# Weight loads of two mixers issued from GpSimd's queue instead of SyncE's

## The chip, the cores and the metric

The program runs on one core of one Trainium2 chip. The metric is the device time of one execution in microseconds; lower is better. The kernel before took 2750.52 us (median of three runs, 2747.89 to 2755.91).

## What is computed

A diffusion backbone of two layers on 1024 latent tokens and 256 context tokens, 1024 wide. Each layer has a mixer (layer 0: windowed attention beside a gated spatial unit; layer 1: latent attention beside a short gated convolution), and then 16 experts, each of which takes the tokens that score highest for it. Cut to the core:

```python
for layer in range(DEPTH):
    m_lat = split((silu(c) @ mod_w[layer] + mod_b[layer])[:, None], 6)      # the modulation
    h = rms_norm(x, norm1_g[layer]) * (1 + m_lat[1]) + m_lat[0]
    y = even_mixer(h, ...) if layer % 2 == 0 else odd_mixer(h, ...)         # projections, attention, output product
    x = x + m_lat[2] * y
    h = rms_norm(x, norm2_g[layer]) * (1 + m_lat[4]) + m_lat[3]
    x = x + m_lat[5] * expert_choice_ffn(h, router_w[layer], w1[layer], w3[layer], w2[layer])
return rms_norm(x, final_g)
```

In layer 0 the context tokens go the same way; in layer 1 they only give keys and values.

## The kernel before

Four stages follow each other: the mixer of layer 0 (`even`, 0 to about 690 us), its experts (to about 1430 us), the mixer of layer 1 (`odd`, to about 2160 us) and its experts. Every weight is loaded as fp32 and split into two fp16 parts (`split_w`, L101: ScalarE writes the high part, VectorE the low one), and products are three fp16 matmuls (`mm3`, L145).

**Queues.** SyncE (SP in the profile) issues two kinds of DMA. One is the bulk loads of weights: `load_split` (L110), the modulation's slabs in `mod_bank` (L205, L208), the experts' first slabs in `first_slabs` (L428), the output weights of layer 1 (L1150), and the experts' other slabs in `slab` (L452). The other is the transposes by DMA (`turn`, L152) of keys, queries, probabilities and outputs, which the mixers need between VectorE and TensorE, and in layer 1 the row loads `fetch` (L1298). GpSimd (POOL) issues the row loads of the first norm (L273) and of the tails (L295), the tails' stores (L311, L316) and the gathers and scatters of the experts; and while the tokens are being chosen it computes the low half of the experts' first slabs itself (`split_first`, L439). Each engine takes its queue in order: an instruction that waits holds up those behind it.

**Order.** The mixers are written as generators that `weave` (L56) advances side by side, and the framework plans each engine's order from a simulated timeline when the kernel is built (L36). A load is planned as early as its buffer is free, unless it is tied: `behind` (L190; "what is traced inside is issued after ins, on its engine") ties the slabs of bank 1 of layer 0 behind `loaded`, the last of the first weights, which SyncE loads (L204, L880), and L1310 ties the experts' slabs 4 to 10 of layer 1 behind the row load of the last tile, which SyncE loads as well:

```python
with tc.issue_after(K["ld"].ins):
    self.first_slabs(1, FS, 11)
```

**Layer 0.** Bank 0 of the modulation (16 slabs of 512 KB) comes first, then `wkv`, `wz` and `sgu_wT`. Then, beside the tiles' norms, projections and attention, banks 1 and 2 in three buffers `c4`, and `ev_wo`. When the projections are done, `then0` issues four expert slabs of 1 MB, and bank 0 of layer 1 follows in eight slabs of 1 MB (`mods1`, L894). Meanwhile VectorE chooses the tokens (`topk`, L345): a first half over tiles 0 to 5 (`r`), and a second half over tiles 6 and 7 (`l`), which needs the affinities that the tail of tile 7 copies at L341; then the context's choice.

**Layer 1.** Low-rank projections of ten tiles beside banks 1 and 2 of the modulation, convolution (24 loads of `wconv`, four of `od_wo`) beside attention, the tails of eight tiles, the choice beside the splits of eleven expert slabs.

Of the kernel before, what the change touches and what calls it, by code (L numbers as in the profile page):

```python
# [22 lines left out]
P = 128  # L23
# [32 lines left out]
def weave(*streams):  # L56
    """streams: (generator, expected sum of its yields, start); advances the one that is least far, start and length 1 being
    where and how fast it runs against the others; a stream that yields a function waits until it is true"""
    live = [[st[0], 0.0, float(st[1]), st[2] if len(st) > 2 else 0.0, None] for st in streams]
    while live:  # L60
        s = min((v for v in live if v[4] is None or v[4]()), key=lambda v: v[3] + v[1] / v[2])
        try:
            r = next(s[0])
            s[4] = r if callable(r) else None
            s[1] += 0.0 if callable(r) else r
        except StopIteration:
            live.remove(s)


class Tag:  # L70
    """one tag of a pool with a fixed number of buffers"""
# [8 lines left out]
class Net:  # L80
    def __init__(self, nc, tc, I, out, dbg=None):
        self.nc, self.tc, self.I, self.out, self.dbg = nc, tc, I, out, dbg or {}
        self.V, self.S, self.T, self.G, self.Y = nc.vector, nc.scalar, nc.tensor, nc.gpsimd, nc.sync

# [6 lines left out]
    def first(self, g, n):  # L91
        """the generator's instructions before the n traced ahead of them that are ready too"""
# [12 lines left out]
    def load_split(self, src, n, sp, raws, step=1024):  # L105
        """src [128, n] in DRAM -> sp [128, 2, n]"""
        for o in range(0, n, step):
            m = min(step, n - o)
            raw = raws([P, step], "raw")
            self.loaded = self.Y.dma_start(raw[:, :m], src[:, o:o + m]).ins  # L110
# [28 lines left out]
    def stats(self, x, n, junk, tag):  # L139
        """1 / rms of the rows; tag: buffers of its own for each caller that runs beside others"""  # L140
# [9 lines left out]
    def turn(self, dst, src):  # L150
        """dst [128, n, 128] <- the n blocks of src [128, n * 128] transposed, 2-byte elements"""
        return self.Y.dma_start(dst, src, transpose=True)  # L152

    def trans(self, src, n, psum, w=P):
        """src [128, n*w] fp32 -> psum tiles [w, 4, 128]"""
# [34 lines left out]
    def behind(self, ins):  # L190
        """what is traced inside is issued after ins, on its engine"""
        return contextlib.nullcontext() if ins is None else self.tc.issue_after(ins)

    def mod_bank(self, l, i, psum, raws, last=None, n=1024):
        """rows 32g + stream of the bank: columns 512(4i + g) of the modulation of layer l; n: columns of a load"""
# [3 lines left out]
        for k in range(9):  # L199
            for c in range(0, 2048, n):  # L200
                slab = raws([P, n], "mslab")
                cols = slice(i * 2048 + c, i * 2048 + c + n)
                if k < 8:
                    with self.behind(last and last[0]):  # L204
                        self.Y.dma_start(slab, I["mod_w"][l, k * P:(k + 1) * P, cols])  # L205
                    lhs, rows = self.cs[:, k, :], P
                else:
                    self.Y.dma_start(slab[0:1], I["mod_b"][l:l + 1, cols])  # L208
# [11 lines left out]
    def mod_cols(self, l, i, g0, psum):  # L220
        """chunks g0, g0 + 1 of a bank with the model's dimension on partitions: psum [128, 4, 128], columns 32(g0 + g) + stream"""
        return self.trans(self.modsb[l, i], 4, psum)[0]

    def mod_AB(self, l, which, psum):
        """per-partition gain and shift [128, 8] of the norm before the mixer (1) or before the experts (2)"""
# [19 lines left out]
    def router(self, l, j, A, B, psum):  # L245
        """router weights with the norm's gain in them, and the row that its shift gives"""
# [12 lines left out]
    def mod_bc(self, l, m, j, dst, psum):  # L259
        """row m of the modulation for stream j on all partitions, over WS"""  # L260
# [7 lines left out]
    def norm_T(self, src, l, j, hi, lo, xs, psum):  # L268
        """hi, lo: [128, 8, 128] views"""
# [18 lines left out]
    def tail(self, l, j, t, src, catT, wout, m2, xd, h2d, aff, psum, c4, t2, cn=None, xin=None, ptr=None):  # L288
        """catT: k -> (hi, lo) [128, 128 tokens]; wout: (k, half) -> (hi, lo); yields its tensor-engine time"""
# [55 lines left out]
    def topk(self, src, n, cap, tag, off=0, alt=None, bufs=0):  # L345
        """largest cap of src [16, n] in falling order and their columns plus off; src is used up; alt: a second buffer, which
        lets the search for columns run beside the next round"""
# [20 lines left out]
    def merge(self, r, l):  # L368
        """largest 128 of two falling lists of 128; on equal values the first list wins"""
# [10 lines left out]
    def slots(self, vals, idf, cap, psum, halves):  # L380
        """per slot: row index and gate [slots, 16]; halves: also the index of half rows, for both halves"""
# [25 lines left out]
    def ring(self, raws, spls, first=()):  # L407
        """buffers for the experts' weights as loaded and split, (pool, tag) of each, no pool: self.ep; first: those for the first loads"""
# [13 lines left out]
    def first_slabs(self, l, a, b):  # L422
        """loads of the weights a .. b before the tokens are chosen"""
        src = [s for e in range(2) for s in [self.I[n][l, e, fh, kh] for fh in range(2) for n in ("w1", "w3") for kh in range(2)]
               + [self.I["w2"][l, e, q] for q in range(4)]]
        for i in range(a, b):
            raw = self.raw()
            self.Y.dma_start(raw, src[i])  # L428
            self.ahead.append((raw, None))

    def split_first(self, a, b, last=None):
        """their split, beside VectorE, which the choice holds; not before the instruction last"""
# [9 lines left out]
    def slab(self, src, a):  # L442
        """128 x 2048 weights, split: two views [128, a, 2048 / a]"""
# [14 lines left out]
    def experts(self, l, xd, h2d, lat, ctx, hook=None, keep=None, out=None):  # L458
        """lat = (idx, gate, _); ctx = (xdc, h2dc, (idx, gate, idx2)) or None"""
# [7 lines left out]
        def halves(name, i, e):  # L467
            """[128, 8, N] for expert e, in self.ep or in a buffer of the pool keep"""
# [42 lines left out]
        def rows(fh, w1, w3, xh, xl, gh, gl):  # L511
            """512 of the hidden columns with the tokens on partitions, then transposed and split"""
# [87 lines left out]
    def norm_out(self, xs, fg, tag):  # L600
        """the rows of the tiles over their rms, times the gain, in place"""
# [16 lines left out]
    def even(self, xd, xdc, h2d, h2dc, then):  # L618
        nc, tc, V, S, T, G, Y, I = self.nc, self.tc, self.V, self.S, self.T, self.G, self.Y, self.I
        with self.pool("m0") as pm, self.pool("m0p", PSUM) as pp:  # L620
# [25 lines left out]
            with self.pool("m0i") as pi:  # L646
# [18 lines left out]
                loaded = self.loaded  # L665

# [10 lines left out]
            def ropes(ps, H, t):  # L677
                """rotated [128, H, 64] fp32, scale undone by the table"""
# [75 lines left out]
            def score(keep, u):  # L754
                """scores of the unit's heads, a bank for each run of blocks, and the transposed probabilities"""
# [38 lines left out]
            def values():  # L794
                """the oldest unit's probabilities times values; after a tile's last ones its heads' outputs"""
# [681 lines left out]
```

## Time and profile before

| | |
|---|---|
| median of three runs | 2750.52 us |
| lowest, highest | 2747.89, 2755.91 us |
| span of the profiled execution | 2750.4 us |
| TensorE, VectorE, ScalarE, GpSimd busy | 2361.6, 2036.0, 1678.1, 337.3 us |

The page gives the profiled execution's span, 2750.4 us, and no time of its own beside it; what lies around the span is therefore taken as nothing, and the span stands 0.1 us under the median. An engine's busy time is the sum of its instructions; idle time before an instruction is put down to what released it. "SPq" is SyncE's queue: it has no busy time, but the time that its instructions took to issue is shown.

### The profile page before, as it was taken

The page shows a single profiled execution, that of the slowest core. Times are in us where ns is not written, and L with a number is a line of the kernel's source. Part 1 is how long each engine was busy: PE and PEld are TensorE (multiplying, and loading weights), DVE is VectorE, ACT ScalarE, POOL GpSimd, SP SyncE. Part 2 cuts the span into 40 slices and gives each one's busy share as a digit, 9 for nine tenths or more (in the row PEclk, how much of TensorE's full clock was granted, in tenths as well). Part 3 has the DMA queues.
Part 4 walks back from the last instruction along what each step waited for, and adds up shares of the span by engine and source line. Part 5 has one row for each costly group of instructions (what it writes and reads, how often), then busy time and mean ns, then how long its engine had stood idle before and what let it go on. Part 6 is the DMA issues. An engine that isn't in the chain of part 4 may idle for free. (4 is left out here: it accounts for less than half of the span.)

```text
span 2750.4 us, 48542 instructions
## 1 busy us (share of the span) xinstructions
PE 2361.6 (86%) x19075; PEld 1436.0 (52%) x19075; DVE 2036.0 (74%) x3886; ACT 1678.1 (61%) x2750; POOL 337.3 (12%) x198
## 2 busy tenths in 40 slices
PE   5889888864899999999989989988884699999995
PEld 1345555432677777776855645544553244444442
DVE  5466666676677777767857768778778789888887
ACT  4355556514666676767745456656554588777774
POOL 1000000003111111111120000000015111112211
PEclk8999999886899999999999999999986799999998
DMA  8775555473788888887967657878876499999997
GB/s 309 218 171 118 123 106 117 93 260 112 267 307 285 323 286 322 289 319 272 352 204 225 147 124 142 152 137 186 162 187 244 181 371 401 361 366 360 373 370 273
DMA packets 461995, 661.32 MB, mean 240 GB/s; under 512 B 371115, under 2 KB 371419, under 8 KB 411077
## 3 DMA queue, kind: packets, MB, share of 16 engines
q1 hardware_dynamic: 439894, 582.81, 66.8%
q0 software_dynamic: 21872, 75.41, 9.4%
q8 instruction: 149, 2.44, 0.4%
q14 instruction: 80, 0.66, 0.1%
HBM read 526.86 MB, written 41.94 MB: 207 GB/s over the span
## 5 line engine op out<-in xcount | busy, mean ns | idle before, releaser
L103 DVE SCALAR_TENSOR_TENSOR spl<-raw,spl 128x2048 f16<-128x2048 f32 x369 | 831.7, 2285 | 149.4 <-ACT spl L102 148.8
L102 ACT ACTIVATE spl<-raw 128x2048 f16<-128x2048 f32 x369 | 690.5, 1910 | 191.7 <-DMA raw<-in_w 73.0
L146 PE MATMUL pb<-xsh,spl 128*128 128x160 f16 x1024 | 222.6, 239 | 0.0
L148 PE MATMUL pb<-xsh,spl 128*128 128x160 f16 x1024 | 222.2, 239 | 0.0
L147 PE MATMUL pb<-xsl,spl 128*128 128x160 f16 x1024 | 222.1, 239 | 0.0
L146 PE MATMUL pa<-xsh,spl 128*128 128x160 f16 x1024 | 215.9, 234 | 0.0
L147 PE MATMUL pa<-xsl,spl 128*128 128x160 f16 x1024 | 215.7, 234 | 0.0
L148 PE MATMUL pa<-xsh,spl 128*128 128x160 f16 x1024 | 215.6, 234 | 0.0
L146 PEld LDWEIGHTS <-spl 128*128 128x128 f16 x2048 | 204.0, 100 | 7.2 <-PE yc L590 5.1
L148 PEld LDWEIGHTS <-spl 128*128 128x128 f16 x2048 | 204.2, 100 | 0.2
L147 PEld LDWEIGHTS <-spl 128*128 128x128 f16 x2048 | 204.0, 100 | 0.2
L146 PE MATMUL y<-spl,gh 128*128 128x512 f16 x512 | 195.2, 383 | 10.2 <-ACT gh L114 10.2
L147 PE MATMUL y<-spl,gh 128*128 128x512 f16 x512 | 195.1, 382 | 0.0
L148 PE MATMUL y<-spl,gl 128*128 128x512 f16 x512 | 189.3, 385 | 4.9 <-DVE gl L116 4.9
L579 POOL DMA_INDIRECT xd<-ysb,idxl x31 | 125.4, 4044 | 529.2 <-DVE ysb L572 503.6
L1212 ACT ACTIVATE pr<-sps,nm 128x512 f32<-128x512 f32 (+1 forms) x192 | 116.7, 611 | 104.2 <-DVE nm L1203 79.5
L146 PE MATMUL po<-vS,pT 128*128 128x64 f16 x976 | 121.9, 198 | 56.7 <-DMA pT<-ps 34.6
L1195 PE MATMUL sps<-kT,qT 128*128 128x512 f16 (+1 forms) x576 | 133.7, 352 | 11.6 <-ACT pr L1212 11.2
L146 PEld LDWEIGHTS <-pT 128*128 128x128 f16 x976 | 92.1, 101 | 89.9 <-DMA pT<-ps 48.6
L1196 DVE TENSOR_REDUCE mx<-sps 128x1 f32<-128x512 f32 (+1 forms) x192 | 112.6, 596 | 33.9 <-PE sps L1195 30.9
L116 DVE TENSOR_TENSOR ps<-pr,ps 128x512 f16<-128x512 f32 (+1 forms) x192 | 111.8, 595 | 34.6 <-ACT ps L114 34.4
L213 PE MATMUL modps<-mslab,cs 128*2 128x512 f32 x384 | 89.4, 681 | 53.1 <-DMA mslab<-in_mod_w 48.6
(439 smaller groups left out, 5957.1 us busy)
## 6 DMA issues: line engine op xcount, KB each, us to landing
raw<-in_w SPq DMA_DIRECT2D x384, 1024.0 KB, 7.6
mslab<-in_mod_w SPq DMA_DIRECT2D x80, 512.0 KB, 5.8
mslab<-in_mod_w SPq DMA_DIRECT2D x8, 1024.0 KB, 9.5
raw<-in_wz SPq DMA_DIRECT2D x12, 512.0 KB, 6.7
raw<-in_wconv SPq DMA_DIRECT2D x24, 256.0 KB, 3.6
xin<-in_x POOLq DMA_DIRECT2D x8, 512.0 KB, 6.1
raw<-in_ev_wo SPq DMA_DIRECT2D x8, 512.0 KB, 3.9
xres<-in_x POOLq DMA_DIRECT2D x8, 512.0 KB, 5.3
```

The lines of the kernel that those rows point to most:

```text
L102: self.S.activation(hi, raw, AF.Copy, scale=scale)
L103: self.V.scalar_tensor_tensor(lo, raw, scale, hi, op0=OP.mult, op1=OP.subtract)
L116: self.V.tensor_tensor(lo, src, hi, OP.subtract)
L146: self.T.matmul(ps, lh, rh, start=first, stop=False)
L147: self.T.matmul(ps, lh, rl, start=False, stop=False)
L148: return self.T.matmul(ps, ll, rh, start=False, stop=last).ins
L213: T.matmul(ps[c0:c0 + 2], lhs, slab[:rows, g * 512:(g + 1) * 512], start=False, stop=(k == 8), tile_position=(0, c0))
L579: G.indirect_dma_start(out=xd, out_offset=IOA(ap=lat[0][:, e:e + 1], axis=0), in_=ysb, in_offset=None, compute_op=OP.add)
L1195: T.matmul(ps[:, :w], qT[:, 4 * j + h % 4], kT[:, k, c0:c0 + w], start=j == 0, stop=j == 2)
L1196: V.tensor_reduce(mx[:, i:i + 1], ps[:, :w], axis=AX.X, op=OP.max)
L1212: S.activation(pr[:, :w], sp[i][:, :w], AF.Exp, bias=nm, scale=SC1, accum_out=dn[:, i:i + 1])
```

## The change

A field `bulk` names the engine that issues the bulk loads. It is SyncE at the start, GpSimd from the point in `even` where the first weights have been issued to the end of that mixer, and GpSimd again in the whole of `odd`. The experts' `slab` and `early`, the row loads `fetch` and the transposes stay on SyncE. (Comments are also taken out.)

```diff
         self.V, self.S, self.T, self.G, self.Y = nc.vector, nc.scalar, nc.tensor, nc.gpsimd, nc.sync
+        self.bulk = self.Y
...
     def load_split(self, src, n, sp, raws, step=1024):
-            self.loaded = self.Y.dma_start(raw[:, :m], src[:, o:o + m]).ins
+            self.loaded = self.bulk.dma_start(raw[:, :m], src[:, o:o + m]).ins
...
     def mod_bank(self, l, i, psum, raws, last=None, n=1024):
                     with self.behind(last and last[0]):
-                        self.Y.dma_start(slab, I["mod_w"][l, k * P:(k + 1) * P, cols])
+                        self.bulk.dma_start(slab, I["mod_w"][l, k * P:(k + 1) * P, cols])
-                    self.Y.dma_start(slab[0:1], I["mod_b"][l:l + 1, cols])
+                    self.bulk.dma_start(slab[0:1], I["mod_b"][l:l + 1, cols])
...
     def first_slabs(self, l, a, b):
-            self.Y.dma_start(raw, src[i])
+            self.bulk.dma_start(raw, src[i])
...
     def even(self, xd, xdc, h2d, h2dc, then):
                 loaded = self.loaded
+            self.bulk = G
...
+        self.bulk = Y
         return lat_slots[0], ctx
...
     def odd(self, ms, mw, xs, xsc, xd, h2d, W, then):
+        self.bulk = G
...
-                            Y.dma_start(raw, I["od_wo"][q])
+                            self.bulk.dma_start(raw, I["od_wo"][q])
...
             K["mo"].__exit__(None, None, None)
+            self.bulk = Y
             return r
```

## Rows read from the trace of the kernel before

**Rows 1.** The page's first lines: span, busy time of each engine.
```profile
span 2750.4 us, 48542 instructions
PE 2361.6 (86%) x19075; PEld 1436.0 (52%) x19075; DVE 2036.0 (74%) x3886; ACT 1678.1 (61%) x2750; POOL 337.3 (12%) x198
```
**Rows 2.** Busy time by stretch: PE, PEld, DVE, ACT, POOL; then PEclk, DMA share, GB/s.
```profile
555.00:629.00 74.00, 53.00 (x322) 24.50 (x322) 50.55 (x123) 12.56 (x23) 3.19 (x6) 0.84 0.68 234
...
2045.00:2122.00 77.00, 48.44 (x219) 28.75 (x217) 64.58 (x128) 43.59 (x38) 35.86 (x14) 0.72 0.71 283
```
**Rows 3.** TensorE's waits, 105 to 200 us: total, times, longest (us).
```profile
PE modps L213 <- DMA mslab<-in_mod_w: 4.0, 4, 2.1
```
**Rows 4.** TensorE's waits, 555 to 629 us.
```profile
PE modps L213 <- DMA mslab<-in_mod_w: 17.6, 1, 17.6
```
**Rows 5.** TensorE's waits, 1432 to 1600 us.
```profile
PE modps L213 <- DMA mslab<-in_mod_w: 17.6, 5, 9.4
PE kvps L146 <- DMA ckT<-hk: 9.1, 2, 6.9
```
**Rows 6.** DMA issues: queue, count, KB each, median us from issue to landing.
```profile
mslab<-in_mod_w SPq DMA_DIRECT2D x80, 512.0 KB, 5.8
xin<-in_x POOLq DMA_DIRECT2D x8, 512.0 KB, 6.1
xx<-xd SPq DMA_DIRECT2D x8, 512.0 KB, 3.6
```
**Rows 7.** SyncE's queue in order of time: start, us to issue.
```profile
48.51 0.33 SPq L110 DMA_DIRECT2D raw<-in_sgu_wT  x1
48.88 1.38 SPq L205 DMA_DIRECT2D mslab<-in_mod_w  x3
...
554.82 2.31 SPq L428 DMA_DIRECT2D raw<-in_w  x4
...
557.75 11.63 SPq L152 DMA_TRANSPOSE pT<-p  x1
...
1400.35 0.90 SPq L110 DMA_DIRECT2D raw<-in_wconv  x2
...
1586.56 1.21 SPq L152 DMA_TRANSPOSE ckT<-hk  x1
...
2080.36 0.33 SPq L1298 DMA_DIRECT2D xx<-xd  x1
```
**Rows 8.** DMA traffic of the first 31 us.
```profile
DMA packets 3211, 10.96 MB, mean 354 GB/s; under 512 B 495, under 2 KB 543, under 8 KB 3211
```
**Rows 9.** VectorE in order of time: start, duration, in brackets idle before.
```profile
602.34 0.21 DVE L365 TENSOR_SCALAR tkir<-tkir 16x128 f32<-16x128 uint32 x1
...
624.82 0.17 DVE L329 TENSOR_REDUCE rnm<-lg 128x1 f32<-128x16 f32 x1 [14.31 <-PE lg L327]
...
628.82 0.28 DVE L341 COPY aff<-affps 16x128 f32<-16x128 f32 x1 [2.96 <-PE affps L340]
...
1586.07 0.43 DVE L116 TENSOR_TENSOR hk<-ck,hk 128x256 f16<-128x256 f32 x1 [0.48 <-ACT hk L114]
...
2088.02 1.27 DVE L306 SCALAR_TENSOR_TENSOR xx<-yps,xx 128x512 f32<-128x512 f32 x2
```
**Rows 10.** GpSimd in order of time, start of layer 1's mixer.
```profile
1438.18 1.06 POOL L273 DMA_DIRECT2D xin<-xc  x2 [2.85 <-DMA xc<-y,idx]
```
**Rows 11.** Groups by line, 2045 to 2122 us, GpSimd and VectorE: count, busy us, mean ns.
```profile
L439 POOL TENSOR_TENSOR spl<-raw,spl 128x2048 f16<-128x2048 f32 x8 | 32.6, 4070 | 39.1 <-ACT spl L438 39.1
L129 DVE SCALAR_TENSOR_TENSOR rstt<-rstt,mst 128x1 f32<-128x1 f32 x9 | 8.5, 948 | 0.1
L334 DVE TENSOR_SCALAR re<-re,rden 128x16 f32<-128x16 f32 x3 | 7.3, 2423 | 0.1
```
**Rows 12.** The rows of tile xin, 1432 to 1560 us: count, ns least/median/most.
```profile
L275 DVE TENSOR_SCALAR xin<-xin,rstdn x10: 745/753/755, 1445.4 to 1546.0; 128x1024 f32<-128x1024 f32 x10
...
L273 POOL DMA_DIRECT2D xin<-xd x8: 527/528/530, 1452.1 to 1532.9; - x8
```

## The prediction

> **What bounds the kernel now.** I read the page's busy times first: TensorE is busy for 86% of the span, VectorE for 74%, and GpSimd, which is to take the loads, for 12% [rows 1]. That share is an average, so I went by stretches next. The experts, more than half of the span, are not touched; what counts is when each mixer hands its choice of tokens to them. Two stretches of the mixers are not TensorE's: in 555 to 629 us, where layer 0 chooses, TensorE is busy for 53.00 of 74 us, and in 2045 to 2122 us, where layer 1 chooses, for 48.44 of 77, while VectorE has 64.58 [rows 2]. Then I read TensorE's waits in the stretches where bulk loads run, since a load or a transpose that comes sooner is worth at most the wait that it ends. They are small: 4.0 us for slabs in 105 to 200 us [rows 3], 17.6 us in one piece in the choice of layer 0 [rows 4], and 17.6 and 9.1 us in the projections of layer 1 [rows 5]. All together 48.3 us, 1.8% of the span, bounds the whole gain from above.
>
> **What moves.** 139 DMAs change queues: 60 in layer 0 (32 slabs of 512 KB and 4 rows of bias, 8 of `ev_wo`, 7 expert slabs, 8 slabs and a row of bias of bank 0 of layer 1) and 79 in layer 1 (36 for banks 1 and 2, 4 `wuq`, 24 `wconv`, 4 `od_wo`, 11 expert slabs). The bytes and the 16 engines that move them stay. A row load costs GpSimd 0.53 us to issue [rows 12], so 139 make 74 us on an engine that is idle for 88% of the span; I cost the issue itself at nothing, covered by that idleness, and at 0.53 us for each load that stands directly before a store or a split that is already due. SyncE gets its issue times back and then holds transposes and the row loads `fetch` alone. On GpSimd's queue the loads are moved in beside the norms' row loads, the tails' stores and, in the choices, the splits. Step by step:
>
> (a) Start. The slabs of bank 1 were tied behind the last first weight, on SyncE: three of them follow it at once, at 48.88 us [rows 7]. The tie holds only on the engine of its argument, so on GpSimd it is gone, and a load goes out when its buffer is free: two `wconv` loads went out at 1400.35 us, some 180 us before the next ones [rows 7]. The three `c4` buffers are free from the start and GpSimd is idle then. So 3 x 524 KB = 1.57 MB join the first 31 us, in which the DMAs moved 354 GB/s [rows 8] and bank 0 is what TensorE waits for: 1.57 MB / 354 GB/s = 4.4 us at most, 0 at least (they might be planned later). I take +3.5, near the upper end, because the row at 1400.35 shows the habit.
>
> (b) Banks 1 and 2 beside the first tiles. Slabs no longer stand behind transposes that wait for VectorE: of the 4.0 us [rows 3] I take -3; between -4.0 and 0, as they now stand behind the norms' row loads.
>
> (c) Choice of layer 0. At 554.82 us SyncE issues four slabs of 1 MB and a slab of the modulation, and the next transpose holds SyncE for 11.63 us [rows 7], while TensorE waits 17.6 us for that slab [rows 4]. The slab stays behind the same 4 MB, so its own wait stays; but the transposes get a queue of their own, and the context's attention can be done sooner. What is it worth? The first half of the choice ends at 602.34 us, the second starts when the affinities are copied at 628.82, and in between VectorE waits 14.31 us for the logits of tile 7 [rows 9], because TensorE, late, runs the context's output products in between. So between -14.3 and 0; I take -5, a third, since TensorE's order must change as well, and the hole before is in part the slab's.
>
> (d) Start of layer 1. At 1438.18 us the two row loads of the context go out [rows 10], and all that follows waits for them. Three slabs of bank 1, planned for the same moment, now stand before them in one queue: again 1.57 MB, 4.4 us at most, 0 if the order is the other way. I take +2, the middle. The slab waits there (17.6 us, [rows 5]) I cost at nothing: TensorE has no other work before those row loads land.
>
> (e) The later waits for transposes in layer 1, 9.1 us [rows 5]. The longest looks like a transpose behind `wconv` loads; but its source is finished at 1586.07 + 0.43 = 1586.50 us [rows 9] and it is issued at 1586.56 [rows 7]. SyncE was not late. I take 0, between -9.1 and 0.
>
> (f) Choice of layer 1. The tie of slabs 4 to 10 behind the last `fetch` is gone in the same way; they can go out some 30 us sooner than 2080.36 us, right behind slabs 0 to 3. The `fetch` then has no loads beside it: it took from 2080.36 [rows 7] to its use at 2088.02 [rows 9], 7.7 us, where such a load takes 3.6 [rows 6]: -4.1. Against that, the splits come sooner. Eight subtractions of 4.07 us ran on GpSimd in 2045 to 2122 us, and in that stretch VectorE's operations on one column took 948 ns and those on 16 columns 2423 ns; all of these are 15.8 us [rows 11], or 2.0 us a subtraction, and they sit in the tails that the choice waits for. Three more subtractions can move into the stretch: 3 x 2.0 = +5.9, at most 3 x 4.07 = +12.2. I take the difference, +2; between -4.1 and +12.2.
>
> Sum: +3.5 - 3 - 5 + 2 + 0 + 2 = -0.5 us. The span is 2750.4, the page has nothing around it, and the median of the runs is 2750.52: 2750.
>
> One question is left, whether a load from GpSimd's queue is itself slower. Rows of the same size say hardly: 6.1 us for `xin` on POOLq, 5.8 for the slabs on SPq [rows 6], and the issue varies between 527 and 530 ns beside a busy VectorE [rows 12]. I take 0 and keep 0.3 us a load as the bound. The Trainium skill, page "SBUF — State Buffer", section "SBUF: two separate sides", speaks against this change: while VectorE runs an operation that uses both of its ports, GpSimd can't write the descriptors of a DMA that it issues, and the transfer seems to be blocked. With that rule the sum would rise by what the third rival below gives; the rows of `xin` do not show it.
>
> **Rivals.** (1) Faster. If SyncE's blocked issue was what kept TensorE's order stretched, (c) gives its whole 14.3, (b) its 4.0, (e) half of its 9.1, against the same 7.5 from (a), (d) and (f): -15.4, 2735 us. For it speaks the 11.63 us that one transpose held SyncE [rows 7]; against it that elsewhere transposes were issued as soon as their source was there, as in (e).
> (2) Slower, by the lost ties. It takes place at two points, the first 31 us and 2045 to 2122 us, and decides if the three slabs go out before bank 0 has landed and if three or more of the later subtractions run before the last tile's affinities: +4.4 + 12.2, less (b)'s 3, 2764 us. For it speaks that VectorE has just 12.4 us free in that stretch [rows 2]; against it the sooner `fetch`.
> (3) Slower, by starved descriptors: each of the 72 slabs of the modulation that TensorE takes one after the other comes 0.3 us later, 21.6 us, 2772 us. The longest operation of the kind in the norms takes 0.753 us [rows 12], so a load could lose more than 0.3, but the landings say not. This is the rule of the page above.
> (4) The change does not do what it says: the transposes waited for VectorE and not for the loads, and nothing moves but the queue's name: 2750 us, the forecast's own number.
>
> **How the numbers follow.** No measurable change, together with rival 4: 0.36, at 2750. Rival 1: 0.31. Rival 2: 0.27, rival 3: 0.06. A change of 0.3%, 8.25 us, is about what a measurement of this kernel can tell from none, so rival 1 counts as faster and 2 and 3 as slower: 0.31, 0.36, 0.33. Every engine's order in the mixers is planned anew, so each case has a spread of its own. The range goes from rival 1 with some more of (e), 2728, to rival 3 with (d) at its bound, 2775. The forecast's own range, with (a) to (f) at their middle halves, is 2742 to 2758.
>
> **What would show it.** (a) right: in the profile after, `mslab` loads on POOLq before 31 us and TensorE's bank 0 ending some 4 us later. (c) right: pT transposes around 558 us that hold SyncE for 1 to 2 us, and affinities at L341 some 5 us earlier against the stage's start; the wait for the slab still there. (d) right: the first `xin` of layer 1 landing later than before. (f) right: slabs 4 to 10 issued near 2050 us, long `rstt` and `re` on VectorE more often than before. Wrong would be a span of either mixer that shrinks or grows by over 8 us; rival 3 would show as POOLq issues well over 0.53 us or slabs landing over 6.1.

## The result, and the profile after

The changed kernel took 2836.41 us (median of four runs, 2832.37 to 2845.27) against 2752.49 us for the kernel before on the same chip: a ratio of 1.0295 with a 95% interval of 1.0273 to 1.0317, some 84 us slower. I had forecast 2750 us, no change, and a range that ended at 2775.

The page's first lines and its queues, answering to [rows 1]:

```profile
span 2843.5 us, 48591 instructions
PE 2384.3 (84%) x19075; PEld 1443.4 (51%) x19075; DVE 2044.3 (72%) x3886; ACT 1692.0 (60%) x2760; POOL 404.4 (14%) x337
...
q1 hardware_dynamic: 421156, 506.08, 56.8%
q0 software_dynamic: 39120, 152.14, 17.4%
```

GpSimd has 67.1 us more, the issues of the moved loads, and 14% is still little. TensorE is busy for 22.7 us more with the same 19075 matmuls. The rest of the 93 us that the span grew is waiting. (The profiled execution is the longest of the four, so its span grew by 9 us more than the median.) Where the time goes is read from GpSimd's queue in order of time, whose loads, stores and gathers mark the tiles (starts in us). One profiled execution differs from another: in four kernels below that keep the order and the time of the kernel before, the marks of layer 0 come up to 12 us later than in its own profile and the last one up to 20, while the pieces between two marks differ by up to 7 us. So it is the pieces that are read:

| mark | before | after | later by |
|---|---|---|---|
| first row load of the latents | 41.89 | 46.64 | 4.8 |
| layer 0, store of tile 0 | 218.34 | 224.99 | 6.7 |
| store of tile 4 | 418.47 | 448.45 | 30.0 |
| store of tile 6 | 558.62 | 587.44 | 28.8 |
| store of tile 7 | 603.44 | 667.3 | 63.8 |
| first gather of layer 0's experts | 668.0 | 725.1 | 57.2 |
| layer 1, first row load | 1438.18 | 1498.06 | 59.9 |
| last row load of its projections | 1532.8 | 1611.8 | 78.9 |
| first gather of layer 1's experts | 2151.8 | 2240.2 | 88.3 |

Four pieces stand out: 23 us in the four tiles up to 448 us, a stretch without a single bulk load; 28 us in the choice of layer 0; 19 us in layer 1's projections, and about 9, little above that spread, from there to the gather. The experts, where nothing moved, take nearly what they took.

The largest single hole is in layer 0's choice. GpSimd's queue and SyncE's there, in order of time (start, us to issue):

```profile
587.44 0.53 POOL L312 DMA_DIRECT2D xd<-xres  x1 [38.47 <-DVE u L740]
588.05 0.53 POOL L296 DMA_DIRECT2D xres<-in_x  x1
588.58 2.09 POOL L429 DMA_DIRECT2D raw<-in_w  x4
590.66 1.56 POOL L206 DMA_DIRECT2D mslab<-in_mod_w  x3
```
```profile
584.88 23.31 SPq L153 DMA_TRANSPOSE pT<-p  x3
608.31 4.14 SPq L153 DMA_TRANSPOSE sT<-vn  x1
```

TensorE in order of time, then the DMA traffic of 588 to 613 us (packets, MB, share of 16 engines by queue; then KB each and median us from issue to landing), and last the same transposes' line for 300 to 400 us, in which no bulk load runs:

```profile
588.06 0.21 PE L147 MATMUL po<-vS,pT 128*128 128x64 f16 x1 [4.01 <-DVE o L818]
...
612.91 0.24 PE L147 MATMUL po<-vS,pT 128*128 128x64 f16 x1 [24.05 <-DMA pT<-p]
```
```profile
q0 software_dynamic: 1296, 8.39, 85.3%
q1 hardware_dynamic: 2216, 0.55, 15.1%
issues: line engine op xcount, KB each, median us to landing
raw<-in_w POOLq DMA_DIRECT2D x4, 1024.0 KB, 11.5
mslab<-in_mod_w POOLq DMA_DIRECT2D x3, 1024.0 KB, 18.8
xres<-in_x POOLq DMA_DIRECT2D x1, 512.0 KB, 6.0
pT<-p SPq DMA_TRANSPOSE x2, 23.4
```
```profile
pT<-p SPq DMA_TRANSPOSE x16, 3.5
```

Read together: within 3.6 us GpSimd issues 7 MB of weights. The transposes have SyncE for themselves, as the change meant, and still two of them take 23.4 us from issue to landing, where larger ones, of ten blocks instead of eight, take 3.5 us (the median of 300 to 400 us; 5.2 there in the kernel before). TensorE stands for 24.05 us on one of them. A queue of its own is no DMA engine of its own: in that stretch the loads had 85.3% of the 16 engines and the transposes 15.1%. Per engine, 1296 / 16 = 81 packets of the loads (6.5 KB on average) went by while 2216 / 16 = 138 small ones of the transposes (0.25 KB) did, about five for three, so the two queues seem to be served by packets, not by bytes, and the queue with the small packets got few bytes. Of the shared engines the Trainium skill says as much, on the page "DMA: Bandwidth & Descriptors", in the section "Issuing engines are not separate DMA queues": DMAs from different engines run on the same 16 DMA engines and interleave, and issuing from several saves only the sequencer's time. The trace agrees: in these 25 us both queues' packets are on the same 16 engines, with 85.3 and 15.1% of their time.

### The profile page after: what moved, and what is told of

Its sections match the earlier page's. It is cut to its first block, busy times and chain, and to the rows that moved or that the text cites. A ratio compares the mean times of both kernels' runs of the same rounds, so it can differ in the third digit from the quotient of the medians.

```text
span 2843.5 us, 48591 instructions
## 1 busy us (share of the span) xinstructions
PE 2384.3 (84%) x19075; PEld 1443.4 (51%) x19075; DVE 2044.3 (72%) x3886; ACT 1692.0 (60%) x2760; POOL 404.4 (14%) x337
## 4 chain that ended last, share of the span: by engine, by line
PE 50%; DMA 17%; DVE 14%; issue 11%; ACT 7%; POOL 1%; SPq 0%; DVEq 0%; POOLq 0%; ACTq 0%
DMA raw<-in_w 6%; DVE spl L104 4%; DMA pT<-p 4%; PE y L149 3%; PE y L147 3%; PE pb L147 3%; PE pb L149 3%; PE pb L148 3%; PE y L148 3%; ACT spl L103 3%; PE pa L148 3%; PE pa L147 3%; PE pa L149 3%; DMA pT<-ps 2%; PE tr L161 2%
## 5 line engine op out<-in xcount | busy, mean ns | idle before, releaser
L580 POOL DMA_INDIRECT xd<-ysb,idxl x31 | 115.1, 3713 | 546.3 <-DVE ysb L573 500.5
```

The lines of the kernel that those rows point to most:

```text
L580: G.indirect_dma_start(out=xd, out_offset=IOA(ap=lat[0][:, e:e + 1], axis=0), in_=ysb, in_offset=None, compute_op=OP.add)
```

## The experiments

Two things need a word. `MOVE` switches the parts of the change one by one (layer 0: banks and `ev_wo`, choice; layer 1: projections, convolution, expert slabs; the two ties). And where a text says "in the order of", the program is traced and planned twice: first as the kernel whose order is wanted, then as the one to be run, with each instruction tied behind the one that stands before it in the first plan on the same engine. Such a tie fixes the order of issue and adds no waiting. An instruction that changed its queue has no place in the other plan and stays free. The traces bear this out: in each such run the work of TensorE, VectorE and ScalarE stands in the wanted order throughout, and `bias_old`, tied so, takes the time of the kernel before.

```diff
+    nc0, by = traced(FIRST)
+    order = [(i.name, i.engine) for b in nc0.main_func.blocks for i in b.instructions if i.name in by]
...
+                for n, e in order:
+                    if by[n].engine == e:
+                        if e in last:
+                            tc.add_manual_dep(by[n], last[e], NO_SYNC, reason="pin")
+                        last[e] = n
+    nc, _ = traced(SECOND, order)
```

Ratios are to the kernel before on the same chip, whose median was 2755.5 to 2757.2 us beside these runs.

### Layer by layer

```diff
     def even(self, xd, xdc, h2d, h2dc, then):
-            self.bulk = G
+            self.bulk = G if MOVE[0] else Y
...
     def odd(self, ms, mw, xs, xsc, xd, h2d, W, then):
-        self.bulk = G
+        self.bulk = G if MOVE[1] else Y
```

`layer0`: 

> Loads on GpSimd in the mixer of layer 0 alone, on SyncE in that of layer 1, everything planned anew. If the two mixers' losses add up as the traces have them (about 60 us lost by the first gather of layer 0's experts, about 30 more by that of layer 1), this gives 2805 to 2820 us under either theory. Under O it can miss that sum by tens of us, since each plan is another; under Q it should not.

`layer1`: 

> Loads on GpSimd in the mixer of layer 1 alone. If the losses add up as the traces have them: 2775 to 2790 us. Under theory O it may miss that by tens of us either way, and layer 0 up to its experts must be as in the kernel before (first gather near 668 us).

Measured: layer 0 alone 2818.94 us, 1.0226 (1.0194 to 1.0259); layer 1 alone 2773.13 us, 1.0056 (1.0033 to 1.0080). The two excesses make 2.8%, the whole change 2.95%: they add up, and three quarters is layer 0. Layer 1 alone came out a little under its range.

### Queue or order

`pool_oldorder` is the changed kernel in the order of the kernel before; `sp_neworder` the mirror, with the loads on SyncE in the changed kernel's order.

> The changed kernel, its 139 loads on GpSimd's queue, but every engine's other instructions are tied into the order that they have in the kernel before; the moved loads alone are free to stand where the planner puts them. Theory O (the 84 us come from the newly planned order of TensorE, VectorE and ScalarE, not from the queue): near the kernel before, 2740 to 2765 us, with the experts of layer 0 starting near 668 us as before. Theory Q (the loads on GpSimd's queue cost the time themselves, as they stand among row loads, stores and splits in one queue in order): 2800 to 2840 us, since the queue is that of the changed kernel.

> The mirror of the run before: all loads on SyncE, the two ties (which had no effect in the changed kernel) left out, and every engine's instructions tied into the order that they have in the changed kernel, but for the 139 loads, which the planner places on SyncE. Theory O: near the changed kernel, 2815 to 2850 us. Theory Q: near the kernel before, 2745 to 2775 us.

Measured: 2813.33 us, 1.0190 (1.0153 to 1.0228), and 2808.91 us, 1.0194 (1.0162 to 1.0225). The first time lies in theory Q's range. The second is 6 us under theory O's range and far over theory Q's. So neither theory holds alone; each is right in one layer. At the first gather of layer 0's experts the old order with the moved loads is 35.0 us late and the new order with the loads on SyncE is 59.9 us late, as late as the changed kernel (57.2). From the first row load of layer 1 to its experts' first gather, the new order loses 1.7 us with the loads on SyncE and 28.4 with them on GpSimd; the old order loses 34.4 with them there. So in layer 1 the queue alone costs 27 to 34 us in these executions (`layer1`, with a plan of its own, loses 15 us by its median, 9 to 22), and in layer 0 the changed kernel pays for its order, while in the old order the queue would have cost 35. By the times, the new order with the loads on SyncE makes 1.94 of the 2.95%, two thirds.

In layer 0 the two kernels of the new order are equally late, but not in the same pieces. With the loads on SyncE that order loses 18.3 us up to the store of tile 0 (6.7 in the changed kernel), 22.7 in the four tiles after it (23.3) and 21.1 in the choice (28.4). Only the four tiles, where no bulk load runs, are a loss of the order alone; in the other pieces the loads still stand among the transposes, in SyncE's queue.

What that order does shows in the four tiles without bulk loads (store of tile 0 to store of tile 4; PE, PEld, DVE, ACT, POOL busy, then PEclk, DMA share, GB/s), in the kernel before, after, and in `sp_neworder`:

```profile
218.34:418.47 200.13, 178.85 (x1428) 107.46 (x1427) 136.69 (x481) 116.81 (x280) 8.01 (x15) 0.93 0.56 115
```
```profile
224.99:448.45 223.46, 191.14 (x1441) 111.44 (x1440) 142.78 (x496) 124.93 (x294) 8.51 (x16) 0.89 0.48 102
```
```profile
236.60:459.50 222.90, 189.81 (x1446) 112.36 (x1445) 142.70 (x496) 125.00 (x294) 8.54 (x17) 0.91 0.50 103
```

The same matmuls to within 1.3%, on either queue 23 us more. TensorE is idle for 223.46 - 191.14 = 32.3 us instead of 21.3, and busy 12.3 us longer, at a mean granted clock of 0.89 instead of 0.93 (a mix of its two levels, 2.4 and 1.2 GHz), after more waits than before. The one that grew is in TensorE's waits of 230 to 450 us of the changed kernel:

```profile
PE po L147 <- DMA pT<-p: 20.0, 12, 5.1
```

In the kernel before the same wait has 8.1 us in 230 to 420 us. The transposes there are no slower (3.5 us at the median in 300 to 400 us, 5.2 before), so the order seems to ask for them sooner.

Is any new plan a worse one? `bias_free` moves nothing but the nine rows of bias, some 40 KB, and has everything planned anew; `bias_old` has the same nine rows in the old order.

```diff
-                    self.bulk.dma_start(slab[0:1], I["mod_b"][l:l + 1, cols])
+                    (self.Y if (l, i) == (0, 0) else self.G).dma_start(slab[0:1], I["mod_b"][l:l + 1, cols])
```

> The kernel before with nothing on GpSimd but the nine rows of bias of the banks (4 or 8 KB each, some 40 KB in all); ties in force, everything planned anew. They move next to nothing, so whatever this differs from the run below with the same nine rows is what another plan is worth. If the planner's order is as good as the kernel before's whatever the change: 2748 to 2762 us. If any change of queue shakes the plan out of a good order (theory O): 2775 to 2815 us.

> The same nine rows on GpSimd, in the order of the kernel before on every engine: the control of the run above. 2748 to 2760 us under every theory.

Measured: 2755.27 us, 0.9994 (0.9974 to 1.0014), and 2759.39 us, 1.0002 (0.9981 to 1.0023). The time did not change. But neither did the plan of layer 0, or hardly: up to its experts' first gather 23 of 3628 matmuls stand at another place in TensorE's order than in the kernel before (told apart by the tiles that they write and read), against 1892 in the changed kernel. In layer 1's mixer 2389 of 4886 do. So a new plan of layer 1 costs nothing by itself, and a change of queue need not disturb the plan of layer 0. Whether another plan of layer 0 would lose time as well, this run doesn't show. The order that loses comes with these loads and, as the next runs show, with the ties.

### The ties

`sp_noties` leaves both ties out and all loads on SyncE. `pool_ties` is the changed kernel with both in force:

```diff
     def norm_T(self, src, l, j, hi, lo, xs, psum):
-        self.G.dma_start(x, src)
+        self.gx = self.G.dma_start(x, src).ins
...
-                    yield from self.mod_bank(0, i, zc, c4, (loaded, K["mm"]) if i == 1 else None)
+                    yield from self.mod_bank(0, i, zc, c4, (self.gx, K["mm"]) if i == 1 else None)
...
-                                with tc.issue_after(K["ld"].ins):
+                                with tc.issue_after(self.gx):
```

(`gx` is also set at the tails' second store.)

> All loads on SyncE as in the kernel before, only the two ties are left out; the planner is free. It prices the ties together with the new plan that their loss brings. Theory L (the lost ties are what spoils the plan of layer 0): the first gather of layer 0's experts 40 to 60 us late, 2790 to 2815 us in all. Theory O without L (the plan goes wrong because the planner costs a load on GpSimd's queue otherwise): only the ties' own price, 2750 to 2765 us, the first slabs after the first weights' loads gone out early and the first row load of the latents about 4 us late.

> The changed kernel with both ties in force again, on GpSimd's own queue: bank 1 stands behind the latest row load of the norms, expert slabs 4 to 10 of layer 1 behind the last stored rows of the tail before. Everything planned anew. Theory L: most of the 84 us come back, 2755 to 2785 us. Theory T (loads on a queue of their own go out as soon as a buffer is free, lie beside the transposes, and those take longer): only the start's 4 us and some of layer 1's choice come back, 2805 to 2835 us.

Measured: 2792.64 us, 1.0140 (1.0099 to 1.0182), and 2817.85 us, 1.0234 (1.0191 to 1.0277). Without ties the kernel before loses 39 us. That is theory L's range, but not its mechanism: the first gather is 16.8 us late, not 40 to 60. Nearly half of the loss is in layer 1, where on SyncE the last tile's row load stands behind all eleven expert slabs and leaves at 2114.89 us; in the changed kernel those slabs are in the other queue. With ties the changed kernel gets back 1.0295 - 1.0234, 0.6% or 17 us (4 to 30 by the two intervals), and the row load at 41.89 us is on time again. The four tiles, store of tile 0 to store of tile 4, in `pool_ties` and in `sp_noties`:

```profile
226.69:426.52 199.83, 177.97 (x1427) 106.80 (x1426) 136.85 (x482) 117.26 (x281) 8.01 (x16) 0.96 0.56 115
```
```profile
229.51:433.88 204.37, 182.05 (x1426) 107.87 (x1425) 136.99 (x482) 117.38 (x281) 8.01 (x15) 0.93 0.57 113
```

With the ties they take what they took, 199.83 us, and without them, but with the loads on SyncE, 204.37. So the 23 us there need both, the lost ties and the loads on GpSimd's queue. The first gather of `pool_ties` is 29.7 us late, 22 of them after the store of tile 4; 15.5 lie between the stores of tiles 5 and 6, where the four expert slabs leave at 528 to 535 us. Layer 1 still loses 24.5 us between its first row load and the gather. Theory L explains a fifth of the loss, not most of it.

### Part by part, in the order of before

`choice0_old`, `banks0_old`, `proj1_old`, `conv1_old` and `first1_old` move one part each.

```diff
-            self.bulk = G
+            self.bulk = G if MOVE[0] & 1 else Y
...
-                tags = itertools.cycle(range(4))
+                tags = itertools.cycle(range(4)); self.bulk = G if MOVE[0] & 2 else Y
```

(and in the same way at three places of `odd`.)

> Only the loads of layer 0's choice (7 expert slabs, bank 0 of layer 1) on GpSimd; all other instructions in the order of the kernel before on every engine. My prediction's step (c): 5 us faster, 2735 to 2752 us. Theory T: the four expert slabs go out when their buffers are free, some 10 us sooner than in the kernel before, in the midst of the transposes of the context's attention; one of those takes about 15 us, and the kernel is 10 to 18 us slower, 2762 to 2772 us.

> Only banks 1 and 2 and the output weights of layer 0 on GpSimd, in the order of the kernel before on every other engine. My prediction's steps (a) and (b): 0 to +1, 2750 to 2755 us. Theory T: +4 at the start (lost tie) and some 12 to 16 us in bank 2, where slabs and transposes lie side by side: 2766 to 2776 us.

> Only the loads of layer 1's projections (banks 1 and 2, wuq) on GpSimd, everything else in the order of before. My prediction's steps (d) and (e): 2750 to 2755 us. Theory T and the lag of TensorE in the run with all loads on GpSimd in that order (it grows by some 17 us between the first row loads of layer 1 and the end of its projections): 2762 to 2774 us.

> Only wconv and od_wo on GpSimd, everything else in the order of before. The prediction gave these no term of their own (0). In the run with all loads on GpSimd TensorE's lag grows slowly, by 7 us, in the stretch where they are loaded: under theory T 2754 to 2764 us, under the prediction 2748 to 2755 us.

> Only the 11 expert slabs of layer 1 on GpSimd, everything else in the order of before. My prediction's step (f): +2, 2748 to 2757 us. From the lag of the run with all loads on GpSimd in that order, which grows by 7 to 13 us in layer 1's choice: 2756 to 2766 us.

| run | median us | ratio, 95% interval |
|---|---|---|
| `choice0_old` | 2774.52 | 1.0062 (1.0042 to 1.0082) |
| `banks0_old` | 2768.47 | 1.0054 (1.0031 to 1.0077) |
| `proj1_old` | 2773.64 | 1.0067 (1.0038 to 1.0096) |
| `conv1_old` | 2767.27 | 1.0038 (1.0018 to 1.0058) |
| `first1_old` | 2760.16 | 1.0019 (0.9998 to 1.0040) |

The five excesses add up to 2.40%; all together in one kernel gave 1.90% (1.53 to 2.28). No part is a gain. Theory T's ranges hold for `banks0_old`, `proj1_old` and `first1_old`; `choice0_old` and `conv1_old` lie 2.5 and 3.3 us above theirs. `first1_old` can't be told from nothing. And the trace of `conv1_old` doesn't show how it loses: from layer 1's first row load to the gather it takes 2.2 us more than the kernel before, and most of what its profiled execution is longer lies ahead of layer 1, where nothing moved.

How a part loses is seen in `choice0_old`. GpSimd's queue, then SyncE's, then TensorE:

```profile
521.22 0.54 POOL L296 DMA_DIRECT2D xres<-in_ctx  x1 [0.28 <-PE ups L149]
521.74 1.05 POOL L429 DMA_DIRECT2D raw<-in_w  x2
525.28 0.53 POOL L429 DMA_DIRECT2D raw<-in_w  x1 [2.48 <-PE ups L149]
527.87 0.53 POOL L429 DMA_DIRECT2D raw<-in_w  x1 [2.06 <-PE vps L149]
```
```profile
523.47 12.93 SPq L153 DMA_TRANSPOSE pT<-p  x2
536.45 5.80 SPq L153 DMA_TRANSPOSE qT<-qq  x3
```
```profile
537.67 0.24 PE L147 MATMUL po<-vS,pT 128*128 128x64 f16 x1 [6.97 <-DMA pT<-p]
```

The four slabs leave 27 to 33 us sooner than in the kernel before, where they went at 554.82 us [rows 7] (the expectation had some 10): as soon as each buffer is free ("<-PE ups" is the matmul that had it). They hit the queries' and probabilities' transposes. Two of these hold SyncE for 12.93 us, and the store of tile 6 comes 15.5 us late.

In bank 2 of `banks0_old` the same happens with smaller loads. DMA traffic of that bank in the kernel before (138 to 175 us) and there (142 to 190 us):

```profile
DMA packets 11124, 8.90 MB, mean 241 GB/s; under 512 B 9518, under 2 KB 9518, under 8 KB 11121
...
mslab<-in_mod_w SPq DMA_DIRECT2D x10, 512.0 KB, 5.9
...
pT<-p SPq DMA_TRANSPOSE x6, 6.2
```
```profile
DMA packets 10266, 8.49 MB, mean 177 GB/s; under 512 B 8714, under 2 KB 8714, under 8 KB 10263
...
mslab<-in_mod_w POOLq DMA_DIRECT2D x10, 512.0 KB, 8.7
...
pT<-p SPq DMA_TRANSPOSE x6, 11.5
```

The same ten slabs and six transposes of `pT` (with five other transposes beside them before and three here); side by side both take longer, and 177 GB/s go where 241 went.

### The moment of the issue

`choice0_late` is `choice0_old` with the slabs held until the moment at which SyncE had sent them; `choice0_later` holds them until the last tail's store; `raws0_later` moves only the four expert slabs, and those as late.

```diff
+                for n, behind in [(slab, store_of_tile_6) for slab in first_four]:
+                    tc.add_manual_dep(by[n], behind, NO_SYNC, reason="pin")
```

> As choice0_old (the loads of layer 0's choice on GpSimd, everything else in the order of before), but the four expert slabs are tied behind the tail's store at 558.6 us and the slabs of bank 0 behind them, so that they go out when they did on SyncE (554.8 us), not when their buffers come free. Theory T, its form in which the moment of the issue decides: the loss is gone, 2745 to 2762 us, and the first gather is at 666 to 674 us. If a load from GpSimd's queue is bad for the transposes at any moment: as choice0_old, 2765 to 2785 us.

> Layer 0's choice on GpSimd, everything else in the order of before; the four expert slabs go out only behind the last tail's store (603 us in the kernel before), bank 0 behind the one before it (559 us). If the transposes of the context's attention are what is late in the choice of the kernel before, too, this beats it: TensorE's hole of 17.6 us shrinks and the second half of the choice starts sooner, 2738 to 2748 us. If VectorE's choice alone sets that stretch: 2748 to 2758 us.

> Only those four expert slabs on GpSimd, behind the last tail's store; bank 0 and all else on SyncE in the order of before. Bank 0's first slab no longer stands behind 4 MB, so TensorE's hole of 17.6 us should be nearly gone, and the transposes behind it have 1 MB to wait for: 2736 to 2747 us if that hole counts, 2748 to 2756 us if VectorE's choice covers it.

Measured: 0.9993 (0.9970 to 1.0016), 0.9994 (0.9974 to 1.0014), 0.9996 (0.9976 to 1.0016). The first says that in the choice GpSimd's queue costs nothing by itself that these runs can tell (0.16% at most): what costs is when the loads go. The other two say that there was nothing to gain either. In `raws0_later` bank 0's slab is early, and TensorE's waits of 540 to 640 us answer to [rows 4]:

```profile
PE tr L161 <- DVE xn L316: 10.2, 1, 10.2
PE modps L214 <- DMA mslab<-in_mod_w: 4.3, 1, 4.3
```

The hole of 17.6 us has shrunk to 4.3, and a wait of 10.2 us for VectorE has come in its place. From the store of tile 6 to the gather it takes 108.4 us, 109.3 in the kernel before. That stretch was VectorE's.

The same test in the changed kernel's own order, `after_later`: only the four expert slabs are held until the store of tile 7.

> The changed kernel in its own order on every engine; only the four expert slabs of layer 0 (4 MB), which stand behind the tail's store at 587.4 us, are tied behind the next tail's store (667 us in the changed kernel). Three slabs of bank 0 (3 MB) stay where they are. Theory T: the transpose that took 23.4 us beside those 7 MB takes some 10 us, TensorE's hole of 24.1 us is cut to about half, and the kernel takes 2818 to 2828 us. If the hole is set by something else in the order: 2832 to 2840 us.

Measured: 2825.12 us, 1.0258 (1.0221 to 1.0295), by the medians 11 us less than the changed kernel, but the two intervals overlap. TensorE's hole, in order of time:

```profile
601.99 0.23 PE L147 MATMUL po<-vS,pT 128*128 128x64 f16 x1 [14.10 <-DMA pT<-p]
```

14.10 us instead of 24.05, with 3 MB beside the transposes instead of 7; as expected. From the store of tile 6 to the gather it takes 127.3 us, against 137.7 in the changed kernel and 109.3 in the kernel before: 10 us come back, and the rest of the choice's loss in that order stays, as it does with all loads on SyncE (130.5 in `sp_neworder`).

### Behind the experts' stores

At the start of layer 1 the loads have another trouble. GpSimd's queue in `proj1_old`:

```profile
1433.46 1.42 POOL L597 DMA_INDIRECT xc<-y,idx  x1 [2.51 <-DVE y L596]
...
1436.65 2.12 POOL L111 DMA_DIRECT2D raw<-in_wuq  x3
1438.22 1.60 POOL L274 DMA_DIRECT2D xin<-xc  x2
1446.08 0.55 POOL L111 DMA_DIRECT2D raw<-in_wuq  x1 [6.26 <-DVE wuq L104]
1446.62 0.53 POOL L206 DMA_DIRECT2D mslab<-in_mod_w  x1
```

`wuq` and the first slab now stand behind the last scatter of layer 0's experts, which waits for VectorE, and the slab stands behind the fourth `wuq`, which waits for its buffer. SyncE had issued `wuq` from 1415.40 us and the slab at 1432.20. `proj1_keep5` leaves these five on SyncE:

```diff
+    def queue(self):
+        self.kept = getattr(self, "kept", 0) - 1
+        return self.Y if self.kept >= 0 else self.bulk
...
     def odd(self, ms, mw, xs, xsc, xd, h2d, W, then):
+        self.kept = 5
```

> As proj1_old (the loads of layer 1's projections on GpSimd, the order of before), but wuq and the first slab of bank 1 stay on SyncE. Theory H (on GpSimd they stand behind the last stores of layer 0's experts, and the first slab comes 12 us late): 7 to 9 us less than proj1_old, 2760 to 2768 us, with TensorE's first matmuls of bank 1 near 1438 us again. Without H: as proj1_old, 2768 to 2780 us.

Measured: 2765.20 us, 1.0028 (1.0008 to 1.0049), against 1.0067 of `proj1_old`. The first matmuls of bank 1 in `proj1_old` and in `proj1_keep5`, answering to [rows 5]:

```profile
1450.63 3.67 PE L214 MATMUL modps<-mslab,cs 128*2 128x512 f32 x8 [19.30 <-DMA mslab<-in_mod_w]
```
```profile
1442.09 1.88 PE L218 MATMUL modps<-mslab,cs 128*2 128x512 f32 x4 [9.38 <-DMA mslab<-in_mod_w]
```

A wait of 19.30 us against 9.38, and 9.4 in the kernel before: theory H holds for the wait, at 10 us. The times differ by 8 to 11 us, though their intervals overlap. In the changed kernel that matmul starts at 1510.54 us, after a wait of 19.71; in `sp_neworder`, with the loads on SyncE, the wait is 15.01, so there about half of the excess comes with the order.

## Why the prediction was wrong

The measured time is 61 us above the range, and the prediction's own sign of being wrong came true twice: the mixers grew by 57 and 28 us where 8 were allowed. Two steps failed.

The larger is "Every engine's order in the mixers is planned anew, so each case has a spread of its own": the new plan was named and got no term in the sum. With the loads on SyncE the changed kernel's order costs 1.94% (1.62 to 2.25), 53 us, all of it by the first gather of layer 0's experts, where it is 59.9 us late.

The other is the sentence under **What moves**, "The bytes and the 16 engines that move them stay", from which I drew only that bandwidth is unchanged, and in (c) that "the transposes get a queue of their own, and the context's attention can be done sooner". The order in one queue had been doing work: it let a load go only after the transposes ahead of it. On a second queue the load goes when its buffer is free, and the transposes share the engines with it. The new queue makes the remaining 1.0%, in layer 1, where part of it is another thing, loads that stand behind scatters (see (d)); and in the order of before it makes all of the 1.90% of `pool_oldorder`.

(a) +3.5, with the tie lost. Right in place and nearly in size: three slabs left at 10.16 to 12.27 us, the last matmuls of bank 0 start at 35.13 us instead of 31.08, and the row load came 4.8 us late, a little over the bound of 4.4. What I left out is what the lost ties do to the plan together with the new queue: with the ties back the four tiles take what they took, and the kernel 17 us less.

(b) -3, between -4.0 and 0. Wrong in sign in the old order, where banks 1 and 2 with (a) cost 15 us. In the changed kernel's order the store of tile 0 was only 6.7 us late, but the wait that was to shrink didn't: from the first row load to that store TensorE waits 9.0 us for slabs, 7.1 before.

(c) -5, between -14.3 and 0. Wrong in sign: +0.62%, 17 us, by itself in the old order, and 28 us between the store of tile 6 and the gather in the changed kernel, 10 of which come back when the four expert slabs are held (`after_later`). I had expected transposes that hold SyncE for 1 to 2 us; three held it for 23.31. The row that should have warned me is the 11.63 us of [rows 7]. I read it as a transpose that stood behind loads in a queue; those loads were in flight, and would have been on any queue. And the gain that I hoped for wasn't there: with the hole cut to 4.3 us, `raws0_later` takes the same time, for VectorE's choice covers them.

(d) +2, at most 4.4. The mechanism was named (the wrong load stands first in one queue), but I looked only at the row loads of the context. The loads themselves stand behind the scatters, which I listed as GpSimd's and didn't count: 10 us of waiting in `proj1_old`.

(e) 0. `proj1_keep5` still costs 0.28%, 8 us. In `proj1_old` the kT transposes land after 10.9 us at the median and the slabs after 9.6 in 1480 to 1516 us, against 5.7 and 6.3 in the kernel before (1472 to 1508 us): as in bank 2. `conv1_old`, with the `wconv` loads to which I gave no term, is 0.38% slower, 10 us; where it loses them its trace doesn't show.

(f) +2. Right as far as it can be told: 1.0019 by itself, and in the changed kernel the lag between the tail of tile 6 and the gather didn't grow.

The costs that I set at nothing: GpSimd's issues of slabs did stay at 0.53 us (0.57 at most), and the 64 slabs of 512 KB on its queue landed after 5.0 us at the median. The same 64 took 5.2 us before; the 5.8 of [rows 6] takes in the 16 slabs of bank 0, which stayed on SyncE. So rival 3, starved descriptors, did not happen. A median said nothing here, though: the loss sits in the few loads that meet transposes. Rival 2, slower by lost ties, had the right sign and the right first place, but is a fifth of the loss. How wide the spread of new plans is, no row of before could have told, and `bias_free` doesn't either, as its plan of layer 0 stayed. Two bounds don't follow from the prediction's own terms, without bearing on the miss: rival 1 with all of (e) gives 2730.5 us, not 2728, and (a) to (f) at their middle halves give 2732 to 2758, not 2742.

Open is why the planner chose that order of layer 0. With the ties, or with the loads on SyncE, it doesn't lose the four tiles; which of the moved loads leads it astray was not separated. Open is also whether the loads on a queue other than GpSimd's would lose as much: no run has them on ScalarE's.

## What to carry to other kernels

Here two queues shared one set of DMA engines, so moving loads off the queue of the transposes didn't protect the transposes; it took away the order that did. Before moving a load, list what it stood behind in its old queue and what it will stand behind in the new one, and check that every tie still names an instruction of its own engine. And before pricing a hole in one engine, ask which other engine ends that stretch: here TensorE's 17.6 us were covered by VectorE, and closing them gave nothing. The waits of a kernel bound what a change can gain, 48.3 us here. They don't bound what it can lose; a new plan, above all, needs a term.

## What was not expected of the hardware

A transpose by DMA took 3.5 us from issue to landing at the median where no bulk load runs (5.2 in the kernel before), and 23.4 us beside 7 MB from the other queue, while the packets of the loads, some 26 times as large, passed three to its five. With transposes and slabs of 512 KB on two queues the DMA engines moved 177 GB/s at a share near 1, where nearly the same transfers in one queue made 241 (bank 2 of `banks0_old`). In the changed kernel's order the DMA engines moved 242 GB/s in that bank (129 to 177 us); what makes the difference is not shown. That the queues are served by packets is worked out from the counts of one stretch, and wasn't tested by itself. None of the versions tried is faster than the kernel before.
